# Six half output projections of a second transformer block, computed beside its attention heads instead of behind them

## The chip, the cores and the metric

One core of a Trainium2 chip runs the whole program. The metric is the device time of one execution in microseconds (us). Times shown for whole runs are medians over executions; times of single instructions come from one profiled execution.

## What is computed

The kernel computes two transformer blocks, of two layers each, over 512 tokens of 1024 features (256 further tokens in a context). What the change touches is the second block's `mixer_out`. Per layer:

```
px = split_cols(hx @ w_in[l])
q = rope_2d(px[0]...); k = rope_2d(px[1]...); v = px[2]
attn = windowed_attention(q, k, v, kc, vc, attn_sink[l])
...
y_conv = conformer_conv(c_a, c_b, conv_w, conv_b, ln_g, ln_b)
y_four = fourier_mix(f_u, w_four, b_four)
y = jnp.concatenate([attn * jax.nn.silu(g_att),        # 512 features: 8 heads of 64
                     y_conv * jax.nn.silu(g_conv),     # 256 features
                     y_four * jax.nn.silu(g_four)], axis=-1)  # 256 features
...
x = x + gate[:, None, :] * (y @ w_out)                 # 1024 -> 1024
```

The attention is over 128-token blocks with their neighbours and the 256 context tokens. In the tail of layer 0 the next layer's context keys and values are also made.

## The kernel before, in words

Activations lie transposed: a tile is 128 features by 512 tokens, so `x` is 8 tiles (`x_135` to `x_142` in the trace) and the concatenated `y` is 8 tiles, `ys[0..3]` from attention (two heads to a tile), `ys[4:6]` from the convolution, `ys[6:8]` from the Fourier part. Every value is kept as a high and a low part (hi, lo), and each product is three matmuls on TensorE (PE): hi by hi (L172), lo by hi (L173), hi by lo (L174). A weight chunk comes by a DMA on SyncE's queue into a `raw` tile (2 buffers). Each 1024 columns of it are then copied into `wh` on ScalarE (ACT, L146), and the rest is subtracted into `wl` on VectorE (DVE, L149); `wh` and `wl` have 3 buffers each.

`layer2` runs twice (l = 0 and 1). After the projections it runs the eight heads, `attn_x`. A head goes through scores (`z` banks), softmax on DVE and ACT, transposes of the probabilities (L1467), the split of these into `pt` hi (ACT) and `pt` lo (DVE), and value products (`b<-pt,Vh` and `b<-pt,Vl`). These steps are 48, and behind step i `more(i)` draws `FILL[i % 6]` steps from a generator, `rest()`, which holds work that doesn't depend on the heads: two gate projections, the Fourier projection, the end of the convolution, and the Fourier transform. It has 20 steps, and FILL gives 24 draws. What a draw emits stands at that place of the program; a scheduler then orders instructions on each engine by a model of the times, and each engine runs its own list in order.

Behind the heads stands `late()` (layer 0: the norm of the context) and then the output projection, `out_proj`. It takes `w_out` in four chunks c of 1 MB. Each gives two outputs j (one tile of `x` each), as 8 inputs by 3 matmuls of 512 columns, and the sum is added to `x` by `upd`, one DVE instruction (L156, `x<-b,ada_c,x`). The inputs come in the order 4, 5, 6, 7, 0, 1, 2, 3. The last chunk runs by halves of the tokens, beside the norm that follows (`ending`); in layer 0 also the next layer's context keys and values (`mid`, `ctx_kv`) are put ahead of it.

Of the kernel before, what the change touches and what calls it, by code (L numbers as in the profile page):

```python
# [15 lines left out]
ALU = mybir.AluOpType  # L16
# [18 lines left out]
FILL = (1, 0, 1, 0, 1, 0)  # L35
# [43 lines left out]
def body(ctx, tc, t, dbg):  # L79
# [55 lines left out]
    # work beside the main line comes behind this instruction of the vector engine  # L135
# [25 lines left out]
    def split(hi, lo, src, scale=None, eng=None):  # L161
        """hi + lo = src * scale; both fit one pass of the tensor engine."""
        if scale is None:
            copy(hi, src)
            tt(lo, src, f(hi), ALU.subtract, eng)
        else:
            copy(hi, src, scale)
            stt(lo, src, scale, f(hi), ALU.mult, ALU.subtract)
# [9 lines left out]
    def warm(n):  # L178
        """Products that nothing reads: they hold the tensor engine's clock up over a short wait."""
# [27 lines left out]
    def wjoin(srcs, n):  # L207
        """The same of several pieces of n columns one behind the other, 1024 columns to a tile."""
# [74 lines left out]
    # masks [q, k]: all; keys after the query; keys at or before it; keys after it. bef: keys before it  # L283
# [39 lines left out]
    def mod_dots(src, pairs, tag="m"):  # L323
        """pairs: (vector, destination column); src: [128, 1024] rows of a transposed weight."""
# [27 lines left out]
    def mods_first(ks):  # L352
        """The first shift and scale, tile by tile."""
# [44 lines left out]
    def rsqrt(v, n):  # L398
        """1 / sqrt(v) of a few columns: a first guess from the bits, and three Newton steps."""
# [10 lines left out]
    def rsqrt_ln(v, n):  # L410
        """1 / sqrt(v): a first guess by exp and ln, and a Newton step."""
# [8 lines left out]
    def rsqrt_act(src, n, over):  # L420
        """1 / sqrt(src / over + eps): a first guess by exp and ln, and a Newton step."""
# [9 lines left out]
    def colsum(tiles, n, fill=0):  # L431
        """sums over the partitions and tiles, tokens on the partitions: [128, n / 128] in PSUM."""
# [9 lines left out]
    def squares(tiles, n, eng=gp):  # L442
        """squares summed over the tiles but the last, and those of the last."""
# [12 lines left out]
    def spread(cols_, n):  # L456
        """[tokens, n / 128] -> [128, n], the same on every partition."""
# [20 lines left out]
    def norm_mod(xs, n, A, sh, dst, sq=None, cols_=None):  # L478
        """dst[k] = (hi, lo) of x * rsqrt(mean x^2 + eps) * A + sh."""
# [16 lines left out]
    class Ending:  # L496
        """The norm of X by halves of the tokens, beside the products that end the phase before."""
# [19 lines left out]
        def pace(self, d, i, at):  # L517
            """The first half's statistics go between the second half's products."""
# [4 lines left out]
    def modulated(A, sh):  # L523
        """An ending that leaves h, and its tiles."""
# [32 lines left out]
    def ffn(l, gu, dn, js, ji, per_f, per_d, h=None, sq=None, first=(), side=None, ending=None):  # L557
# [40 lines left out]
        if ending:  # L598
            # the last two outputs together, by halves of the tokens
# [18 lines left out]
    def positions():  # L618
# [8 lines left out]
        # angles, reduced to [-pi, pi]  # L627
# [18 lines left out]
        # distance of the one key that each merged column stands for: own block up to the query,  # L646
        # the block before past it
# [61 lines left out]
    def proj_gen(src, h, n, done):  # L709
        """The same step by step, handed to done at the end."""  # L710
# [11 lines left out]
    def proj_n(srcs, h, width, ntt):  # L722
        """token-major: [tokens, width] per 128 tokens."""
# [23 lines left out]
    def vtile(p):  # L747
        """hi and lo of a pair's values [keys, first | zeros | second], by 128 keys."""
# [5 lines left out]
    def v_evac(v, i, src, scale=None):  # L754
        """src [128, 128]: two heads of 64 go to columns 0 and 128 of 192."""
# [23 lines left out]
    def stick(r, q, k, v, po):  # L779
        """One head, half r of a pair: q, k (hi, lo) [128, 512]; scores as [key, query]."""  # L780
        rr = slice(r * 64, r * 64 + 64)
        za, zb, zc = (bank("z") for _ in range(3))
        # key block -> bank, its place there, and in the split parts
# [91 lines left out]
    def window_out(p, S, v, O):  # L875
        # transposed, by key block: queries of the same block, then of the next one
# [29 lines left out]
    def latent_proj(l, g, w3, cq, ckv, skv, ekv, kper, v, qk):  # L906
        """Queries and keys of two heads, normed and rotated; their values into v."""
# [63 lines left out]
    def latent_scores(q, k):  # L971
        """The probabilities of one head: by query block, over the keys up to it."""
# [17 lines left out]
    def latent_probs(E):  # L990
        """Transposed: by key block (hi, lo) over the queries from it on."""
# [22 lines left out]
    def rope(x, cg, sg, nh):  # L1014
        """x: [128, 2, nh, 32] in place; cg, sg: [128, 2, 32]."""
# [22 lines left out]
    def group_norm(O, l, base, over, mix):  # L1038
        """mix[i]: (hi, lo) made over the outputs themselves."""
# [8 lines left out]
    def out_proj(src, l, y, n, ks, after, upd, cs=range(4), ending=None, mid=None):  # L1048
        """ks: the inputs in the order in which they come; no weight is fetched before `after` is issued."""
# [24 lines left out]
    def mixer(l, h, ending):  # L1074
# [5 lines left out]
        def nb():  # L1080
            # values and window keys, token-major
# [22 lines left out]
        def sp(p):  # L1104
            # stick-breaking queries and keys, transposed
# [20 lines left out]
        def na():  # L1126
            # window queries and the shared rotated key part, token-major
# [503 lines left out]
    def layer2(l, rot, kc, vc, side, late, h, ending, mid=None):  # L1631
# [84 lines left out]
        def upd(d, ps, c):  # L1716
            stt(X[d][:, c], ps, MOD2[l, 2, "c2"][:, d:d + 1], X[d][:, c], ALU.mult, ALU.add)
# [189 lines left out]
```

## Time and profile before

| | us |
|---|---|
| median of 3 runs | 2899.38 |
| lowest and highest run | 2892.01, 2900.29 |
| span of the profiled execution | 2898.8 |
| PE busy in it (14059 instructions) | 2767.1 (95%) |
| weight loads of PE (PEld, overlapping PE) | 2332.3 (80%) |
| DVE busy | 1820.6 (63%) |
| ACT busy | 1151.5 (40%) |
| POOL busy | 511.9 (18%) |

The span is that of one execution under the profiler, and lies 0.6 us under the median. A busy share is over the whole span; what binds in one stretch is read from that stretch.

### The profile page before, as it was taken

How to read it: one execution, taken by the hardware profiler on the slowest of the kernel's cores; microseconds unless marked ns; L12 is line 12 of the kernel's file. 1: busy time of each engine (PE TensorE's matmuls, PEld its weight loads, DVE VectorE, ACT ScalarE, POOL GpSimd, SP SyncE). 2: the span in 40 equal slices, each digit the busy share in tenths (PEclk: the TensorE clock that was granted, in tenths of full speed). 3: DMA queues.
4: the chain of work that ended last, by engine and by line, in shares of the span. 5: the costliest groups of instructions: out<-in, count | busy, mean ns of one | idle time of the engine just before them, and what ended most of it. 6: DMA issues, size and time to landing. Idle time of an engine off the chain costs nothing.

```text
span 2898.8 us, 37037 instructions
## 1 busy us (share of the span) xinstructions
PE 2767.1 (95%) x14059; PEld 2332.3 (80%) x14059; DVE 1820.6 (63%) x3330; ACT 1151.5 (40%) x2231; POOL 511.9 (18%) x663
## 2 busy tenths in 40 slices
PE   7989999989999999999999899999999999999998
PEld 5767888778888888888888778888888977787776
DVE  7898965466666647743344766833487956559554
ACT  3333425655422334222345654222336234442352
POOL 3153411243000011000112421000012022211220
PEclk9999999979999999999999899999999988999899
DMA  7623362003467644532220023632233411122001
GB/s 266 222 82 107 128 236 75 29 8 117 162 239 247 234 164 137 186 123 102 80 97 29 15 95 124 223 104 102 84 128 105 150 36 36 59 88 73 35 30 58
DMA packets 69873, 334.40 MB, mean 115 GB/s; under 512 B 7872, under 2 KB 12224, under 8 KB 50112
## 3 DMA queue, kind: packets, MB, share of 16 engines
q1 hardware_dynamic: 69696, 332.05, 33.2%
q8 instruction: 110, 1.80, 0.2%
q14 instruction: 67, 0.55, 0.1%
HBM read 327.30 MB, written 4.72 MB: 115 GB/s over the span
## 4 chain that ended last, share of the span: by engine, by line
PE 79%; DVE 12%; ACT 3%; DMA 3%; issue 2%; POOL 0%; SPq 0%; DVEq 0%; POOLq 0%; ACTq 0%
PE b L173 17%; PE b L172 17%; PE b L174 17%; PE z L172 8%; PE z L174 7%; PE z L173 7%; DVE bacc L156 3%; DMA mraw<-wmod 3%; DVE wl L149 2%; PE z L438 1%; DVE mraw L156 1%; ACT s L129 1%; PE b L1467 1%; PE z L816 1%; DVE s L156 1%
## 5 line engine op out<-in xcount | busy, mean ns | idle before, releaser
L146 ACT ACTIVATE wh<-raw 128x1024 fp32r<-128x1024 f32 (+4 forms) x451 | 437.1, 972 | 756.3 <-PE b L173 365.0
L172 PE MATMUL b<-hh,wh 128*128 128x512 f32 (+1 forms) x1856 | 687.7, 378 | 17.6 <-DVE s L149 5.0
L174 PE MATMUL b<-hh,wl 128*128 128x512 f32 (+1 forms) x1856 | 693.3, 376 | 4.9 <-DVE wl L149 4.9
L149 DVE TENSOR_TENSOR wl<-raw,wh 128x1024 fp32r<-128x1024 f32 (+3 forms) x431 | 495.2, 1150 | 302.1 <-ACT wh L146 293.7
L173 PE MATMUL b<-hl,wh 128*128 128x512 f32 (+1 forms) x1742 | 668.4, 385 | 6.5 <-DVE hl L156 5.7
L172 PEld LDWEIGHTS b<-hh,wh 128*128 128x128 f32 x1856 | 348.7, 190 | 82.2 <-DVE s L149 5.5
L174 PEld LDWEIGHTS b<-hh,wl 128*128 128x128 f32 x1856 | 353.2, 190 | 68.6 <-DVE wl L149 7.4
L173 PEld LDWEIGHTS b<-hl,wh 128*128 128x128 f32 x1742 | 331.5, 190 | 71.9 <-DVE hl L156 8.8
L149 POOL TENSOR_TENSOR s<-s,s 128x512 f32<-128x512 f32 (+3 forms) x74 | 91.8, 1242 | 1178.6 <-ACT s L447 1070.5
L156 DVE SCALAR_TENSOR_TENSOR mraw<-mraw,c 128x1024 f32<-128x1024 f32 x192 | 236.7, 1244 | 86.6 <-DMA mraw<-wmod 80.4
L174 PE MATMUL z<-a,wl 128*128 128x512 f32 x638 | 251.3, 395 | 12.3 <-DVE wl L149 12.3
L172 PE MATMUL z<-a,wh 128*128 128x512 f32 x638 | 249.8, 393 | 3.2 <-ACT a L146 3.0
L173 PE MATMUL z<-a,wh 128*128 128x512 f32 x638 | 250.1, 393 | 0.0
L172 PE MATMUL b<-a,wh 128*128 128x256 f32 (+1 forms) x480 | 155.3, 326 | 8.1 <-ACT wh L146 6.7
L129 ACT ACTIVATE s<-b 128x512 f32<-128x512 f32 x87 | 51.8, 596 | 277.2 <-PE b L174 277.2
L174 PE MATMUL b<-a,wl 128*128 128x256 f32 (+1 forms) x480 | 155.2, 327 | 0.4 <-POOL wl L149 0.2
L174 PEld LDWEIGHTS z<-a,wl 128*128 128x128 f32 x638 | 120.9, 190 | 42.5 <-DVE wl L149 17.6
L149 DVE TENSOR_TENSOR s<-s,b 128x512 f32<-128x512 f32 x87 | 59.5, 684 | 136.7 <-PE b L174 117.5
L172 PEld LDWEIGHTS z<-a,wh 128*128 128x128 f32 x638 | 121.0, 190 | 28.7 <-ACT a L146 4.0
L173 PE MATMUL b<-a,wh 128*128 128x256 f32 (+1 forms) x440 | 140.5, 320 | 1.9 <-DVE a L149 1.9
L173 PEld LDWEIGHTS z<-a,wh 128*128 128x128 f32 x638 | 120.9, 189 | 25.4
L153 POOL TENSOR_SCALAR s<-s,tiny 128x256 f32<-128x256 f32 (+1 forms) x160 | 89.1, 572 | 285.0 <-DVE tiny L1376 133.2
(366 smaller groups left out, 5071.4 us busy)
## 6 DMA issues: line engine op xcount, KB each, us to landing
raw<-gu SPq DMA_DIRECT2D x88, 1024.0 KB, 4.9
mraw<-wmod SPq DMA_DIRECT2D x144, 512.0 KB, 4.7
raw<-dn SPq DMA_DIRECT2D x64, 704.0 KB, 4.2
raw<-wt SPq DMA_DIRECT2D x27, 1024.0 KB, 4.9
mraw<-wada SPq DMA_DIRECT2D x48, 512.0 KB, 4.0
raw<-wout SPq DMA_DIRECT2D x20, 1024.0 KB, 5.0
raw<-wq SPq DMA_DIRECT2D x6, 1024.0 KB, 5.0
raw<-wnb SPq DMA_DIRECT2D x4, 1024.0 KB, 4.9
```

The lines of the kernel that those rows point to most:

```text
L129: i = act_eng.activation(out, in_, func, **kw)
L146: return act_eng.activation(out, in_, AF.Copy, scale=scale)
L149: return (eng or dve).tensor_tensor(out=out, in0=a, in1=b, op=o)
L153: (eng or dve).tensor_scalar(out=out, in0=a, scalar1=s1, scalar2=s2, op0=o1, **kw)
L156: return dve.scalar_tensor_tensor(out=out, in0=a, scalar=s, in1=b, op0=o0, op1=o1, **kw)
L172: pe.matmul(out, wh, xh, start=start, stop=False, **kw)
L173: pe.matmul(out, wh, xl, start=False, stop=False, **kw)
L174: lastmm[0] = pe.matmul(out, wl, xh, start=False, stop=stop, **kw)
L438: lastmm[0] = pe.matmul(ps[:, i:i + 1], a[:, i * 128:(i + 1) * 128], one, start=m + i == 0, stop=True, skip_group_check=True)
L816: pe.matmul(b[:, c], ntri if jj == j else nones, a, start=False, stop=True, skip_group_check=True)
L1467: last = pe.transpose(pt[:, n * 128:n * 128 + 128], src, ident)
```

## The change

`FILL` becomes (1, 0, 1, 0, 1, 1), so that 32 draws are made. `rest()` gets 7 more steps. One is empty. The other 6 are the part of chunks c = 0, 1, 2 of the output projection that belongs to inputs 4 to 7 (convolution and Fourier tiles): for each c one load of 512 KB, one hi copy and one lo subtraction of 1024 columns, and for each of two outputs 12 matmuls and an `upd` of its own. Behind the heads `out_proj` takes only inputs 0 to 3 for these chunks (loads of 512 KB, one copy and one subtraction each); chunk 3 stays as it was. Comments and docstrings are removed as well, which moves line numbers and nothing else.

```
-FILL = (1, 0, 1, 0, 1, 0)
+FILL = (1, 0, 1, 0, 1, 1)
...
             yield from fourier_gen(l, fu, 512, gates[2:4], ys[6:8], "dft512",
                                    lambda i: (hslot("h", i % 4), hslot("l", i % 4)))
+            yield
+
+            for c in range(3):
+                w = wload(t["wout2"][l * 4 + c][:, 1024:2048], [(0, 1024)])[0]
+                for j in range(2):
+                    ps = bank()
+                    for i in range(4):
+                        mm3(ps, cut(w, slice(None), slice(i * 256 + j * 128, i * 256 + j * 128 + 128)), ys[4 + i],
+                            i == 0, i == 3)
+                    upd(2 * c + j, ps, slice(None))
+                    yield
+
+        def upd(d, ps, c):
+            stt(X[d][:, c], ps, MOD2[l, 2, "c2"][:, d:d + 1], X[d][:, c], ALU.mult, ALU.add)
 
         fill = rest()
...
         run(fill)
-
-        def upd(d, ps, c):
-            stt(X[d][:, c], ps, MOD2[l, 2, "c2"][:, d:d + 1], X[d][:, c], ALU.mult, ALU.add)
-
         late()
-        out_proj("wout2", l, ys, 512, (4, 5, 6, 7, 0, 1, 2, 3), after, upd, ending=ending, mid=mid)
+        out_proj("wout2", l, ys, 512, (0, 1, 2, 3), after, upd, (0, 1, 2))
+        out_proj("wout2", l, ys, 512, (4, 5, 6, 7, 0, 1, 2, 3), after, upd, (3,), ending=ending, mid=mid)
```

How this moves instructions is seen at three places, all in layer 1 (in layer 0 they read alike). The first is PE's list between the value products of head 5 (`b_23484` before, `b_23560` after) and the transposes of a later head. Before:

```order
L173 MATMUL b_23484<-pt_23700,Vh_3887_21772 128x384
L174 MATMUL b_23484<-pt_23700,Vl_3888_21773 128x384
L1467 MATMUL b_23852<-ident,s_23564 128x128
L1467 MATMUL b_23852<-ident,s_23605 128x128 x2
L1467 MATMUL b_23852<-ident,s_23632 128x128
L172 MATMUL b_23484<-pt_23722,Vh_3887_21772 128x384
```

After (`b_23896` and `b_23973` are the fourth and the fifth of the six new groups of 12 matmuls):

```order
L173 MATMUL b_23560<-pt_23847,Vh_3896_21790 128x256
L174 MATMUL b_23560<-pt_23847,Vl_3897_21791 128x256
L174 MATMUL b_23896<-a_4129_23273,wl_23856 128x512
L172 MATMUL b_23896<-a_4131_23275,wh_23855 128x512
L173 MATMUL b_23896<-a_4132_23276,wh_23855 128x512
L174 MATMUL b_23896<-a_4131_23275,wl_23856 128x512
L172 MATMUL b_23973<-a_4123_23255,wh_23969 128x512
L173 MATMUL b_23973<-hl_4124_23256,wh_23969 128x512
```

Twelve products of 512 columns follow one another for each new group, where transposes and value products alternated. All six groups stand ahead of the last value product of the last head.

The second place is DVE's list in the same stretch. Before (`pt` are lo halves of probabilities, `tiny` pieces of softmax sums, `s<-b` a pair of heads' output times its gate):

```order
L149 TENSOR_TENSOR pt_23722<-b_23718,pt_23722 128x384
L149 TENSOR_TENSOR pt_23731<-b_23728,pt_23731 128x256
L149 TENSOR_TENSOR pt_23857<-b_23852,pt_23857 128x512
L156 SCALAR_TENSOR_TENSOR s_23737<-b_23484,a_3977_22445 128x512
L149 TENSOR_TENSOR tiny_23752<-tiny_23752 128x1
```

After:

```order
L156 SCALAR_TENSOR_TENSOR x_136<-b_23820,ada_2_c_15444,x_136 128x512
L149 TENSOR_TENSOR pt_23838<-b_23834,pt_23838 128x384
L149 TENSOR_TENSOR pt_23847<-b_23844,pt_23847 128x256
L156 SCALAR_TENSOR_TENSOR x_137<-b_23859,ada_2_c_15444,x_137 128x512
L156 SCALAR_TENSOR_TENSOR s_23873<-b_23560,a_3986_22463 128x512
L149 TENSOR_TENSOR tiny_23888<-tiny_23888 128x1
L156 SCALAR_TENSOR_TENSOR x_138<-b_23896,ada_2_c_15444,x_138 128x512
```

Each group's `upd` stands among them; that of group 2 stands ahead of two lo halves of probabilities, and waits for its group's last product.

The third place is ACT's list where the heads end: the last hi copies of probabilities (`pt`), the copy of the last attention tile (`a<-s`), and the copies of weights. Before:

```order
L146 ACTIVATE pt_23987<-b_23983 128x384
L146 ACTIVATE pt_23996<-b_23993 128x256
L146 ACTIVATE a_4277_24004<-s_24002 128x512
L146 ACTIVATE wh_24010<-raw_24008 128x1024
L146 ACTIVATE wh_24014<-raw_24008 128x1024
```

After:

```order
L146 ACTIVATE pt_24107<-b_24103 128x384
L146 ACTIVATE pt_24116<-b_24113 128x256
L146 ACTIVATE wh_24130<-raw_24128 128x1024
L146 ACTIVATE a_4301_24124<-s_24122 128x512
L146 ACTIVATE wh_24164<-raw_24162 128x1024
```

The first product behind the heads reads `wh_24014` before, the second copy behind the attention tile's, and `wh_24130` after, which stands ahead of that tile's copy. On PE the first four products behind the heads read `wh`, and the fifth reads `wl`, before and after. In layer 0 one more place changes: before, the remaining products of chunk 2 and the warming products stood between the last use of the weight buffer that `ctx_kv` takes and `ctx_kv`'s first product; after, that product stands directly behind the last product of chunk 2, which frees the buffer.

## Rows read from the trace of the kernel before

**Rows 1.** The profile's page: busy time by engine, and the chain that ended last.

```profile
PE 2767.1 (95%) x14059; PEld 2332.3 (80%) x14059; DVE 1820.6 (63%) x3330; ACT 1151.5 (40%) x2231; POOL 511.9 (18%) x663
...
PE 79%; DVE 12%; ACT 3%; DMA 3%; issue 2%; POOL 0%; SPq 0%; DVEq 0%; POOLq 0%; ACTq 0%
```

**Rows 2.** Windows: heads of layers 0 and 1, dense products, two like stretches.

```profile
core 0: us, PE busy (x) PEld busy (x) DVE busy (x) ACT busy (x) POOL busy (x), PEclk, DMA share, GB/s
2351.00:2509.00 158.00, 153.17 (x725) 119.93 (x724) 85.08 (x208) 70.97 (x184) 31.57 (x49) 0.86 0.08 28
...
2682.30:2833.50 151.20, 146.89 (x731) 115.33 (x730) 84.95 (x209) 70.28 (x184) 31.50 (x48) 0.91 0.09 30
...
2841.00:2869.00 28.00, 28.00 (x125) 23.21 (x124) 8.65 (x9) 7.71 (x10) 5.47 (x4) 1.00 0.17 63
...
2451.00:2461.00 10.00, 10.00 (x32) 7.37 (x32) 4.72 (x15) 2.77 (x9) 3.41 (x6) 0.50 0.00 1
2782.00:2792.00 10.00, 10.00 (x57) 7.65 (x57) 6.53 (x20) 5.51 (x19) 3.41 (x6) 0.97 0.00 0
```

**Rows 3.** Waits of PE during the heads of layer 0: total us, times, longest.

```profile
PE b L173 <- DVE pt L149: 1.9, 1, 1.9
PE b L172 <- ACT pt L146: 1.6, 4, 0.7
PE z L172 <- ACT s L129: 0.7, 2, 0.6
```

**Rows 4.** Timeline of PE around the end of the heads, layers 0 and 1.

```profile
2508.65 0.29 PE L174 MATMUL b<-pt,Vl 128*128 128x256 f32 x1
2512.28 0.50 PE L172 MATMUL b<-a,wh 128*128 128x512 f32 x1 [3.34 <-ACT wh L146]
...
2833.22 0.28 PE L174 MATMUL b<-pt,Vl 128*128 128x256 f32 x1
2836.84 0.52 PE L172 MATMUL b<-a,wh 128*128 128x512 f32 x1 [3.34 <-ACT wh L146]
```

**Rows 5.** Timeline of ACT where the heads of layer 0 end.

```profile
2506.81 0.84 ACT L146 ACTIVATE pt<-b 128x384 fp32r<-128x384 f32 x2 [0.65 <-PE b L1467]
2509.70 0.63 ACT L146 ACTIVATE a<-s 128x512 fp32r<-128x512 f32 x1 [2.05 <-DVE s L156]
2510.24 2.94 ACT L146 ACTIVATE wh<-raw 128x1024 fp32r<-128x1024 f32 x3
```

**Rows 6.** Timeline of DVE at the same place.

```profile
2507.34 0.89 DVE L149 TENSOR_TENSOR pt<-b,pt 128x384 fp32r<-128x384 f32 x2 [0.59 <-ACT pt L146]
2508.98 0.69 DVE L156 SCALAR_TENSOR_TENSOR s<-b,a 128x512 f32<-128x512 f32 x1 [0.75 <-PE b L174]
2511.31 3.73 DVE L149 TENSOR_TENSOR wl<-raw,wh 128x1024 fp32r<-128x1024 f32 x3 [1.64 <-ACT wh L146]
```

**Rows 7.** Groups by form, 2834 to 2882 (three) and heads of layer 0 (last).

```profile
L149 DVE TENSOR_TENSOR wl<-raw,wh 128x1024 fp32r<-128x1024 f32 x8 | 9.9, 1251 | 9.2 <-ACT wh L146 9.0
L146 ACT ACTIVATE wh<-raw 128x1024 fp32r<-128x1024 f32 x8 | 8.2, 1053 | 5.1 <-PE b L173 5.1
L156 DVE SCALAR_TENSOR_TENSOR x<-b,ada_c,x 128x512 f32<-128x512 f32 x6 | 4.5, 751 | 14.5 <-PE b L174 14.5
...
L149 DVE TENSOR_TENSOR pt<-b,pt 128x512 fp32r<-128x512 f32 x16 | 11.0, 685 | 9.1 <-ACT pt L146 8.8
```

**Rows 8.** DMA issues in 2430 to 2530: KB each, median us to landing.

```profile
raw<-wout SPq DMA_DIRECT2D x4, 1024.0 KB, 4.9
ctx<-ctx_d SPq DMA_DIRECT2D x2, 512.0 KB, 4.0
```

**Rows 9.** Timeline of PE, the first product of `ctx_kv` in layer 0.

```profile
2554.70 0.39 PE L172 MATMUL b<-hh,wh 128*128 128x256 f32 x1 [0.58 <-ACT wh L146]
```

## The prediction

> **What bounds the kernel now.** I read the page first: PE is busy 95% of the span and holds 79% of the chain that ended last [rows 1]. So the first question is what PE has to do and the second where it stands still. The change neither adds nor removes matmuls; it moves 144 of them (2 layers x 3 chunks x 2 outputs x 4 inputs x 3 products), all of 512 columns, from behind the heads to beside them. Such a move can only gain what PE loses in the heads now, or what it loses where the heads end.
>
> I read three views on that. The windows: the heads of layer 0 take 158.00 us with PE busy 153.17, those of layer 1 take 151.20 with 146.89 [rows 2]. So 4.83 and 4.31 us are plainly idle. The chain of waits says on what: in layer 0 one wait of 1.9 us on a lo half of probabilities (`pt`, DVE), four on hi halves (ACT, 1.6 together), two on exponentials (0.7) [rows 3]. The timeline where the heads end: the last value product starts at 2508.65 and runs 0.29, and the next product waits 3.34 us for a weight copy on ACT; layer 1 shows the same 3.34 [rows 4].
>
> Busy is not the same as full there. Behind the heads, 125 dense products take 28.00 us, 0.224 us each, with weight loads (PEld) busy 23.21, a share of 0.829, at a granted clock of 1.00. In the heads PEld is busy 119.93 of 158.00 (0.76) and 115.33 of 151.20 (0.76), at mean clocks of 0.86 and 0.91; one stretch of 10 us runs at 0.50, and a like stretch of layer 1 gets through 57 products instead of 32 at 0.97 [rows 2].
>
> **The change, part by part.**
>
> *Behind the heads* 144 products of 0.224 us go: −32.3 us. This is sure, since that stretch is full (PE busy 28.00 of 28.00).
>
> *Beside the heads* the same products come back, +32.3 us, less what the heads absorb. The lower bound is nothing: the visible waits lie where no group stands, or new ones replace them. The upper bound comes from the weight loads: at the dense stretch's share of 0.829, layer 0's loads would fit into 119.93 / 0.829 = 144.7 us and layer 1's into 115.33 / 0.829 = 139.1, which leaves 13.3 and 12.1 us, 25.4 together. I take the plainly idle time, 4.83 + 4.31 = 9.1 us. Not each of those waits will have a group in front of it: in layer 1's order the six groups stand close to one another, in the last third of PE's list of the heads. But that is where the 1.9 us wait lies, and groups of twelve dense products should also give back some of the stretches at half clock, which are not in the 9.1. More I don't take, because the dense groups go mostly to a part that already runs near full clock, where a product costs its 0.224.
>
> The Trainium skill, page "Perfetto Trace Analysis", section "Identifying the Most-Contended Engine", says that the busy share of matmuls is not a good measure of how near PE is to its limit, and that MFU and the busy share of weight loads are to be used. By the busy share the heads are 97% full and could take 9.1 us; by the page's measure they are at 0.76 against 0.83 and could take 25.4. The second is a rival below.
>
> *The wait where the heads end.* Now the chain is: last value product, output times gate on DVE (2508.98, 0.69), attention tile's copy on ACT (2509.70, 0.63), then two weight copies, 1.04 each as 2.94 us hold three with overlap [rows 5, 6], and the first product needs the second copy. After the change the first product needs one copy that stands ahead of the attention tile's. It can start when the last hi half of probabilities is done, 2506.81 + 0.84 = 2507.65 [rows 5], and takes 1.05 [rows 7]: 2508.70, before the last value product ends (2508.94). So four products run at once, 0.90 us, and the fifth waits for `wl` on DVE: 0.04 + 0.69 for the output times gate [rows 6] and 1.25 for the subtraction [rows 7], 1.98 − 0.90 = 1.1 us. A wait of 3.34 becomes 1.1: −2.2 twice, −4.4. It rests on the 512 KB being there; a load of that size lands in 4.0 us [rows 8], and its buffer is free as soon as the second of the three new loads beside the heads has been split, some groups earlier. If it is not there, the term is nothing.
>
> *`ctx_kv` in layer 0.* Its first product waits 0.58 for a weight copy now [rows 9]. After the change the buffer of that copy comes free two products before `ctx_kv`: 1.05 − 0.22 = 0.8 us at least, +0.3.
>
> *What I cost at nothing.* Each layer's heads get 3 weight copies on ACT (1.05), 3 subtractions on DVE (1.25) and 6 `upd` of 0.75 [rows 7]: 3.2 us on ACT, busy 70.97 of 158.00, and 8.3 us on DVE, busy 85.08 [rows 2]. The 6 further `upd` per layer are real work, 4.5 us, hidden as long as PE doesn't wait for DVE. The cover is that PE has other products in its list between an `upd`'s group and the value products that read a lo half behind that `upd`. If the cover is gone, a value product waits for the group's last product to be added and its own lo half to be made: 0.04 + 0.75 + 0.69 = 1.5 us a group [rows 6, 7]. DMA: three loads of 1 MB become six of 512 KB per layer; SyncE's queue has nothing else to issue in the heads but the loads of the same generator, and DMA engines are busy 8 to 9% of the time there [rows 2], so 4.0 instead of 4.9 us each [rows 8] is hidden. That more draws are made moves the older steps of the generator a little forward; no product is added by it.
>
> *Sum:* −32.3 + 32.3 − 9.1 − 4.4 + 0.3 = −13.2 us, against the profiled span of 2898.8: 2885.6. The median lies 0.6 over that span: 2886.2 us, −0.46%.
>
> **The rivals.**
>
> *The heads have no room.* PE's idle time stays as it is, because each group lands where PE had work, and what it displaces waits as before. For it: 97% busy, and groups next to one another. Against it: the wait of 1.9 us is for a lo half that stood behind softmax sums, and twelve products now stand about there. Then only the end counts, −4.4 + 0.3: 2894.7, as a run 2895.3. That is 0.14% faster, less than the 0.3% that a measurement of this kernel can tell from no change.
>
> *DVE becomes what PE waits for.* An `upd` waits for its group's last product, in order, and lo halves queue behind it. For it: DVE's list shows `upd` ahead of two lo halves, and lo halves already make PE wait 1.9 us once [rows 3]. Against it: DVE is idle 73 of 158 us, and PE's list has products of the next group between. If each of the 12 groups costs its 1.5 us and nothing is absorbed: 2894.7 + 17.8 = 2912.5, as a run 2913.1, slower by 0.47%. It decides from about 9 of the 12 groups on (−4.1 + 9 x 1.5 = +9.2 us, over 0.3%, which is 8.7).
>
> *The heads are as empty as their weight loads say.* The dense groups bring the clock to full and fill the pipeline, and 25.4 us are absorbed: 2898.8 − 25.4 − 4.1 = 2869.3, as a run 2869.9, −1.0%. For it: half-clock stretches like that of [rows 2] would vanish if PE has dense work in them. Against it: transposes and value products are short, and their loads may not overlap as well as in a dense stretch whatever stands between; and where layer 0 ran at 0.50, the like stretch of layer 1 ran at 0.97, so it is not the lack of work alone.
>
> **How the numbers follow.** The forecast (partly absorbed, 5 to 16 us of 25) gets 0.55, with its own range 2879 to 2890. No room gets 0.22, the empty heads 0.12, DVE in the way 0.11. The range reaches from the lower half of the third rival's time to a little past no room: 2874 to 2899. Faster by over 0.3% (below 2890.7) takes the forecast but for its upper end, and the third rival: 0.52 + 0.12 = 0.64. Within 0.3%: the rest of the forecast, no room, and a few groups' worth of DVE's waits: 0.28. Slower: 0.08, the last part of DVE in the way.
>
> **What will show it.** Right, if after the change the heads are longer by about 11 to 12 us each (158 to some 170, 151 to some 162), PE idle there falls under 2 us or its mean clock rises, the 1.9 us wait on `pt` lo is gone, and where the heads end PE runs four products, then waits 1.1 us for `wl`. No room: heads longer by 16 us each. DVE in the way: waits of PE on `pt` lo halves of 1 to 1.5 us, once per group. Empty heads: longer by 4 us only, clock near 1.00 and PEld share above 0.8. I am wrong altogether if the clock falls in the heads where it was full before: at 0.50 the stretch above did 32 products for 57, and 20 us of such a stretch cost some 9 us, as much as all that I take as absorbed.

## The result

The changed kernel takes 2865.75 us (median of 4 runs, 2864.03 to 2866.28); beside it the kernel before took 2899.84. The ratio is 0.9887, with a 95% interval from 0.9861 to 0.9913: faster by 1.1%, 25 to 40 us. A second set of runs on another chip gave 2866.5 us and 0.9913 (0.9890 to 0.9935). The forecast was 2886.2 us, range 2874 to 2899: the direction was right, the gain more than twice what was forecast, and the time lies under the range.

The page of the changed kernel, its first part:

```profile
span 2864.6 us, 37064 instructions
...
PE 2744.2 (96%) x14059; PEld 2319.6 (81%) x14059; DVE 1825.4 (64%) x3342; ACT 1150.9 (40%) x2231; POOL 511.0 (18%) x663
```

The same 14059 matmuls were busy for 2767.1 us before [rows 1] and are busy for 2744.2 now. Work that is only moved doesn't shrink; it runs faster. The windows of the changed kernel say where. In order: heads of layer 0, heads of layer 1, what lies behind layer 1's heads, what lies behind layer 0's (columns as in [rows 2]).

```profile
2351.70:2508.60 156.90, 154.66 (x798) 124.83 (x798) 90.40 (x216) 74.89 (x188) 31.42 (x49) 0.95 0.10 31
2664.00:2820.40 156.40, 154.41 (x803) 124.94 (x803) 90.59 (x217) 74.79 (x190) 31.39 (x48) 0.96 0.09 31
2820.40:2864.60 44.20, 33.72 (x208) 30.11 (x206) 21.05 (x40) 10.70 (x19) 7.47 (x5) 0.88 0.25 84
2508.60:2664.00 155.40, 149.34 (x843) 128.72 (x842) 122.19 (x213) 58.83 (x111) 30.62 (x32) 0.97 0.28 94
```

And the two stretches behind the heads before the change, layer 1 and layer 0, in the same view:

```profile
2833.50:2898.80 65.30, 52.10 (x281) 44.99 (x280) 24.53 (x43) 15.12 (x23) 7.21 (x5) 0.89 0.19 65
2509.00:2682.30 173.30, 165.24 (x914) 142.04 (x915) 125.13 (x215) 63.71 (x115) 29.68 (x32) 0.97 0.25 86
```

The heads of layer 0 hold 73 matmul records more than before [rows 2] and take 156.90 us instead of 158.00; those of layer 1 hold 72 more and take 156.40 instead of 151.20. So 32.3 us of products came in and the heads grew by 4.1: 28.2 us were absorbed. Behind the heads 17.9 and 21.1 us went. With 0.7 us of a later start the sum is the −34.2 us between the two spans.

What was absorbed is seen in two columns. Idle time of PE (length less busy) fell from 4.83 and 4.31 to 2.24 and 1.99, by 4.9 us. And the granted clock rose from 0.86 and 0.91 to 0.95 and 0.96. At a granted clock of 0.50 ("half clock", 1.2 of 2.4 GHz) products of 512 columns start 0.43 us apart in the kernel before, at 1.00 they start 0.23 us apart. So time lost to half clock can be worked out as (1 − clock) x length: it was 22.1 and 13.6 us and is 7.8 and 6.3, 21.6 us less. 4.9 + 21.6 = 26.5 of 28.2; the rest is within the rounding of the clock to hundredths. This compares one profile with one profile; what the runs as a whole say stands behind the experiments.

The waits of PE in the heads of layer 0 after the change (total us, times, longest), where [rows 3] showed one of 1.9 us:

```profile
PE b L172 <- ACT pt L146: 0.7, 1, 0.7
PE b L173 <- DVE pt L149: 0.5, 2, 0.3
PE z L172 <- ACT s L129: 0.5, 1, 0.5
PE b L1467 <- DVE hl L149: 0.3, 1, 0.3
```

The timeline of PE where the heads end, layers 0 and 1, and at the first product of `ctx_kv`; these answer to [rows 4, 9].

```profile
2508.29 0.29 PE L174 MATMUL b<-pt,Vl 128*128 128x256 f32 x1
2508.42 0.39 PE L172 MATMUL b<-a,wh 128*128 128x512 f32 x1
...
2510.57 0.50 PE L174 MATMUL b<-a,wl 128*128 128x512 f32 x1 [1.08 <-DVE wl L149]
...
2822.30 0.50 PE L174 MATMUL b<-a,wl 128*128 128x512 f32 x1 [1.09 <-DVE wl L149]
...
2533.92 0.39 PE L172 MATMUL b<-hh,wh 128*128 128x256 f32 x1 [0.92 <-ACT wh L146]
```

The first products run as soon as the last value product is issued, and the fifth waits 1.08 and 1.09 us for its `wl`, where 1.1 was forecast. `ctx_kv` waits 0.92, where 0.8 was.

### The profile page after: what moved, and what is told of

Read it like the earlier page. It is cut to its first block, busy times and chain, and to the rows that moved or that the text cites. A ratio compares the mean times of both kernels' runs of the same rounds, so it can differ in the third digit from the quotient of the medians.

```text
span 2864.6 us, 37064 instructions
## 1 busy us (share of the span) xinstructions
PE 2744.2 (96%) x14059; PEld 2319.6 (81%) x14059; DVE 1825.4 (64%) x3342; ACT 1150.9 (40%) x2231; POOL 511.0 (18%) x663
## 4 chain that ended last, share of the span: by engine, by line
PE 77%; DVE 13%; DMA 4%; ACT 3%; issue 2%; POOL 1%; SPq 0%; DVEq 0%; POOLq 0%; ACTq 0%
PE b L173 16%; PE b L172 16%; PE b L174 16%; PE z L172 8%; PE z L174 7%; PE z L173 7%; DVE bacc L156 3%; DMA mraw<-wmod 3%; DVE wl L149 2%; DVE mraw L156 2%; PE z L438 2%; DMA mraw<-wada 1%; PE b L1467 1%; PE z L816 1%; ACT s L129 1%
## 5 line engine op out<-in xcount | busy, mean ns | idle before, releaser
L173 PEld LDWEIGHTS z<-a,wh 128*128 128x128 f32 x638 | 120.9, 189 | 25.4
```

The source lines that it names most:

```text
L173: pe.matmul(out, wh, xl, start=False, stop=False, **kw)
```

## Where half clock came from

Two views of the kernel before show what PE did before its granted clock fell. First, stretches in the windows: one ahead of a fall and one behind it in the heads of layer 1, and one behind the wait of 3.34 us where layer 0's heads end.

```profile
2747.80:2751.80 4.00, 4.00 (x18) 2.37 (x16) 2.99 (x9) 1.91 (x4) 0.73 (x2) 1.00 0.00 0
2751.90:2758.60 6.70, 6.70 (x18) 4.61 (x18) 1.37 (x4) 2.71 (x10) 0.69 (x1) 0.50 0.00 0
...
2512.90:2516.30 3.40, 3.27 (x9) 2.06 (x8) 2.14 (x2) 2.73 (x9) 2.36 (x2) 0.50 0.36 87
```

The third is the plain case: PE stood still for 3.34 us and, 0.6 us after it went on, ran at half clock. The first two are not: PE was busy 4.00 of 4.00 us at full clock, and then ran at half clock for 6.70 us, again with no gap. The groups of the first stretch, by form, say with what it was busy:

```profile
L172 PE MATMUL z<-a,a 64*128 64x384 f32 x2 | 0.9, 442 | 0.0
L173 PE MATMUL b<-hl,wh 128*128 128x512 f32 x2 | 0.8, 394 | 0.0
L173 PE MATMUL z<-kc,a 64*128 64x256 f32 x2 | 0.7, 332 | 0.0
L172 PE MATMUL z<-kc,a 64*128 64x256 f32 x2 | 0.7, 329 | 0.0
L173 PE MATMUL b<-pt,Vh 128*128 128x384 f32 x1 | 0.6, 570 | 0.0
L174 PE MATMUL z<-kc,a 64*128 64x256 f32 x2 | 0.6, 278 | 0.0
```

Ten of the 18 are score products of 64 rows and 256 or 384 columns (`z<-a,a`, `z<-kc,a`); 4 have 512 columns. This is what PE did before the fall, not what set the fall off: since 2732 it had been busy for at least 1.99 of every 2 us with products of the same kinds, at a clock of 1.00. After the change the clock doesn't fall where the heads end, with 1.08 and 1.09 us of waiting (windows of the changed kernel):

```profile
2509.00:2512.50 3.50, 2.42 (x11) 1.67 (x10) 2.99 (x3) 2.81 (x6) 2.42 (x3) 1.00 0.94 317
2820.40:2824.00 3.60, 2.51 (x11) 1.78 (x10) 3.06 (x3) 1.58 (x2) 1.53 (x1) 1.00 0.25 40
```

## The experiments

Theory A: products of 512 columns among the short ones of the heads hold the granted clock up, and what they save there is the part of the gain that the forecast lacks. Rival B: it is FILL, that is the new spacing of the older steps (gates, Fourier) beside the heads. Each run is compared with runs of the kernel before on the same chip (medians 2895 to 2897 us). "Clock" of a run is the mean over the whole span; "lost" below is (1 − mean clock) x median time.

**FILL alone.**

```
-FILL = (1, 0, 1, 0, 1, 0)
+FILL = (1, 0, 1, 0, 1, 1)
```

> The kernel before with the new FILL alone; no product is moved. Theory A (the moved dense products keep the granted clock of TensorE up in the heads, and that is where 20 of the 33 us come from): the heads stay as they were, 158 and 151 us within 4 us, and the whole run stays at 2893 to 2901 us. Rival B (it is the new spacing of the older steps beside the heads that removes the stretches at half clock): the heads fall by 10 to 14 us each, and the run to 2872 to 2880 us.

Measured: 2884.0 us (2873.7 to 2890.1), ratio 0.9953 (0.9930 to 0.9977). The windows of its heads:

```profile
2351.50:2505.80 154.30, 150.65 (x725) 120.69 (x724) 83.22 (x207) 70.81 (x184) 31.42 (x49) 0.86 0.08 28
2680.40:2819.90 139.50, 135.59 (x723) 108.76 (x722) 83.77 (x207) 70.63 (x184) 31.30 (x48) 0.96 0.09 31
```

Neither expectation held: the run lies between them. Layer 0 keeps its clock of 0.86, layer 1 goes to 0.96. The spacing alone is worth 0.5%, 11 us (7 to 20 by the interval), which is some 40% of the gain in the first set of runs and half of that in the second, and A alone is refuted.

**The change with the old FILL** (24 draws, so the last steps are emitted behind the heads).

```
-FILL = (1, 0, 1, 0, 1, 1)
+FILL = (1, 0, 1, 0, 1, 0)
```

> The change with the old FILL: the products are moved, but the last three of the seven new steps are emitted behind the last step of the heads, and the groups stand late. Theory A: the groups crowd into the last two heads, so stretches at half clock that lie earlier in the heads stay; between 8 and 20 us of the 32 are absorbed, and the run takes 2872 to 2885 us. Rival B (spacing of the older steps): with the old spacing the heads absorb their idle time of some 9 us only, and the run takes 2884 to 2892 us.

Measured: 2881.1 us, 0.9940 (0.9921 to 0.9959), inside A's range. Moving the products without the spacing is worth 0.6%, and 0.6 and 0.5 add up to the whole. It is not a clean half, though: in this run's profile the late groups also stand where PE waited when the heads end, and PE doesn't stand still there in either layer, where the changed kernel waits 1.08 and 1.09 us.

**Unread products at the same places, nothing removed** (in `rest()` of the kernel before, with the new FILL).

```
+            yield
+            for c in range(3):
+                for j in range(2):
+                    ps = bank()
+                    for i in range(4):
+                        yh, yl = ys[4 + i]
+                        for m, x in enumerate((yh, yl, yh)):
+                            pe.matmul(ps, identr, x, start=i + m == 0, stop=i + m == 5)
+                    yield
```

> The kernel before with the new FILL, and at the places of the six new groups of a layer 12 products of 512 columns that nothing reads, of a constant tile against the convolution and Fourier tiles: no load, no split, no update, and nothing is taken away behind the heads. 144 products, 32.3 us at 0.224, are added to the program. Theory A: the heads take about as long as after the change (157 us each), so that the run takes 2899 to 2907 us in spite of them. If the heads have no room for products (the gain would come from elsewhere), they take 16 us more each, and the run 2925 to 2933 us.

Measured: 2905.1 us, 1.0028 (1.0009 to 1.0046), inside A's range. The windows of its heads:

```profile
2347.30:2510.20 162.90, 161.24 (x798) 129.37 (x796) 83.52 (x208) 71.74 (x184) 31.40 (x49) 0.91 0.08 27
2685.40:2837.90 152.50, 150.75 (x796) 121.28 (x795) 83.62 (x208) 71.57 (x184) 31.28 (x48) 0.98 0.08 28
```

32.3 us of useless products made the heads 6.2 us longer than before, and the whole run by 0.28%, about 8 us. So the heads absorb products as such, whatever is taken away behind them. Against FILL alone they cost 21 us of 32.3, so 11 are absorbed.

The same two profiles show where. The stretch at the end of the heads, layers 0 and 1, in which the groups stand: FILL alone, then with the unread products, then the changed kernel.

```profile
2474.00:2505.80 31.80, 29.45 (x142) 23.72 (x140) 17.29 (x43) 16.69 (x46) 7.82 (x13) 0.79 0.01 2
2792.00:2819.90 27.90, 25.36 (x132) 20.21 (x130) 16.43 (x41) 15.42 (x41) 7.69 (x12) 0.88 0.00 1
...
2470.20:2510.20 40.00, 39.64 (x212) 31.99 (x210) 17.25 (x44) 17.31 (x45) 7.93 (x13) 1.00 0.01 2
2797.90:2837.90 40.00, 39.62 (x212) 31.94 (x210) 17.22 (x44) 17.26 (x44) 7.76 (x12) 1.00 0.00 1
...
2469.50:2508.60 39.10, 38.87 (x213) 32.10 (x212) 22.45 (x50) 19.31 (x48) 7.85 (x13) 1.00 0.05 16
2781.20:2820.40 39.20, 38.97 (x214) 32.15 (x214) 22.49 (x50) 19.34 (x48) 7.78 (x12) 1.00 0.04 14
```

With the products the clock is 1.00 there, read or unread; without them it is 0.79 and 0.88, which costs 6.7 and 3.3 us, and PE is idle for 4.9 us instead of 0.7. Ahead of the groups none of the 144 products stands. The kernel before has no groups; it is cut here at the last 31 us of its heads, and those are the two last lines. The part ahead, before and after:

```profile
2351.00:2478.00 127.00, 124.81 (x577) 96.72 (x576) 66.28 (x169) 55.12 (x147) 26.77 (x41) 0.84 0.08 26
2682.30:2802.00 119.70, 117.98 (x579) 91.76 (x578) 65.74 (x171) 53.62 (x146) 26.82 (x41) 0.90 0.08 29
...
2351.70:2469.50 117.80, 115.79 (x587) 92.74 (x587) 67.95 (x167) 55.58 (x141) 23.57 (x36) 0.93 0.11 37
2664.00:2781.20 117.20, 115.43 (x591) 92.79 (x591) 68.10 (x168) 55.45 (x143) 23.61 (x36) 0.94 0.11 37
...
2478.00:2509.00 31.00, 28.36 (x150) 23.21 (x149) 18.81 (x40) 15.85 (x38) 4.80 (x8) 0.94 0.11 37
2802.00:2833.50 31.50, 28.91 (x153) 23.57 (x152) 19.21 (x39) 16.66 (x38) 4.68 (x7) 0.95 0.10 34
```

So most of the 21.6 us of the profiled pair lies where only older steps were shifted (32.3 us lost before, 15.3 after; with FILL alone 18). How much is the shift and how much the run can't be told from two profiles: with the changed kernel's order in that part the same loss was 12 us in its second profile and 24 in the profile without updates (both below).

**One chunk, two chunks, four chunks moved.** In the first two the other chunks stay behind the heads with all eight inputs; in the third, chunk 3 is moved like the others and runs behind the heads with inputs 0 to 3, and the place of the next norm's statistics among its products is set anew. The cut shows the first.

```
-            for c in range(3):
+            for c in range(1):
...
-        out_proj("wout2", l, ys, 512, (0, 1, 2, 3), after, upd, (0, 1, 2))
-        out_proj("wout2", l, ys, 512, (4, 5, 6, 7, 0, 1, 2, 3), after, upd, (3,), ending=ending, mid=mid)
+        out_proj("wout2", l, ys, 512, (0, 1, 2, 3), after, upd, (0,))
+        out_proj("wout2", l, ys, 512, (4, 5, 6, 7, 0, 1, 2, 3), after, upd, (1, 2, 3), ending=ending, mid=mid)
```

> The change for chunk 0 alone: two groups per layer beside the heads, chunks 1 and 2 behind them as before. Behind the heads 48 products go, 10.8 us, and 4.4 us of the waits where the heads end. Theory A: two groups already break some of the stretches at half clock, so the heads stay as long as they were or get shorter, and the run takes 2875 to 2886 us. If the gain goes in proportion to the products: a third of the 28 us in the heads, the run 2884 to 2888 us.

> The change for chunks 0 and 1: four groups per layer beside the heads. With the new FILL alone 0.47% was gained, with one chunk moved 0.82%, with three 1.13%. Theory A (the first groups win most, since they take the stretches at half clock away, and later ones cost their full price): two chunks come close to three, 0.95 to 1.15%. If every chunk brings the same: 0.9%.

> The changed kernel with the same part of chunk 3 moved too: eight groups per layer beside the heads, 48 products of 512 columns' worth fewer behind them (10.8 us). Theory A: the heads now run at 0.95 to 0.96 of the clock with 2 us idle, so nearly nothing is left to absorb; the heads grow by 4.5 to 5.4 us each and the run stays within 4 us, 2862 to 2869. If the heads still have room as before the change, another 6 to 9 us are gained: 2857 to 2860.

Measured: one chunk 2875.4 us, 0.9918 (0.9890 to 0.9946), at the edge of A's range; two 2871.6, 0.9924 (0.9898 to 0.9951), a median under both expectations; four 2869.7, 0.9927 (0.9900 to 0.9955), a little beyond A's range. Windows of the heads with one chunk:

```profile
2356.90:2504.30 147.40, 144.71 (x751) 116.10 (x751) 85.63 (x210) 72.90 (x186) 31.36 (x49) 0.94 0.09 30
2671.10:2818.30 147.20, 144.63 (x750) 116.25 (x750) 86.50 (x210) 73.28 (x186) 31.26 (x48) 0.94 0.09 29
```

With 24 products more per layer the heads are 10.6 and 4.0 us shorter than before. From here to three chunks (156.90 and 156.40) 48 more products per layer cost 9.5 and 9.2 us, 0.19 to 0.20 each, nearly their price; against the changed kernel's second profile (152.50 and 157.80, below) they cost 5.1 and 10.6, so the price is not settled. The first chunk, with the spacing, takes most of the gain; between one, two, three and four the intervals overlap. That two come as close to three as A says is neither shown nor refuted.

**A little unread work in the kernel before, old FILL** (in `more(i)`, 4 products behind every sixth step, 64 in the program).

```
+            if i % 6 == 5:
+                a = getattr(lastmm[0], "ins", lastmm[0])
+                ps = bank()
+                for _ in range(4):
+                    m = pe.matmul(ps, identr, swm, start=True, stop=True)
+                    order(getattr(m, "ins", m), a)
```

> The kernel before with its old FILL, and 4 products of 512 columns that nothing reads behind every sixth step of the heads: 64 in the program, 14.3 us at 0.224. No older step is moved in the program. Theory A: they shorten the stretches at half clock in the heads (44 and 27 us before) by about as much as they cost, and the run stays within 5 us of the kernel before. Rival B (only the spacing of the older steps matters): the run gets 12 to 15 us longer, 0.4 to 0.5%.

Measured: 2896.1 us, 1.0008 (0.9982 to 1.0034). 14.3 us of products cost nothing that can be measured (the interval is 5 us less to 10 us more). The heads in its profile, which is one of its faster runs:

```profile
2358.10:2505.20 147.10, 142.29 (x755) 111.83 (x755) 83.57 (x208) 71.14 (x184) 31.89 (x49) 0.99 0.09 30
2679.80:2824.70 144.90, 141.48 (x753) 111.81 (x753) 84.73 (x208) 71.20 (x184) 31.70 (x48) 0.99 0.09 30
```

Seven of a layer's eight groups of 4 stand in the heads (30 and 22 records more, since some are missing in a trace), the last behind the last value product, where PE then waits 2.42 us instead of 3.34. The heads are 10.9 and 6.3 us shorter than before, at a clock of 0.99. No older step of the program was moved. This shows A's mechanism by itself: dense products among the short ones pay for most of their price through the clock (some 10 us in the table below), and for a little of it in the wait where the heads end. (The other runs of this kernel had a mean clock of 0.969 against 0.972 in the profiled one, so 0.99 is its good case.)

**The same in the changed kernel**, all over the heads, and only behind the third and the sixth step.

> The changed kernel with 4 products that nothing reads behind every sixth step of the heads, the places at which they cost the kernel before nothing: 64 in the program, 14.3 us. Theory A says that here they cost most of their price, since the moved products already hold the clock: at most the 7 to 17 us of half clock left per layer can be won, 3 to 8 us of time each. The run takes 2865 to 2875 us. Were they free here too, whatever the clock does, it would stay at 2864 to 2868.

> The changed kernel with 4 products of 512 columns that nothing reads behind the third and behind the sixth step of each layer's heads: 16 in the program, 3.6 us at 0.224. They stand at the two places at the start of the heads where half clock remains after the change (7 to 17 us a layer in its two profiles). Theory A (such products hold the granted clock): these stretches shrink by more than half, and the run is 3 to 8 us shorter than the changed kernel, 2858 to 2863 us. Rival (what is left there follows from a wait of TensorE, and products only shift it): 2866 to 2871 us.

Measured: all over the heads 2878.8 us, 0.9948 (0.9928 to 0.9968), 13 us over the changed kernel: here they cost nearly their price of 14.3, a little beyond what A allowed. The mean clock of these runs is the highest of all (0.973), and 8 us came back through it, as A allowed. But beside the clock the runs are 20 us longer, more than the products' price; 2 us of that is more idle time in the heads, the rest is open. At the start only: 2870.8 us, 0.9915 (0.9892 to 0.9938), no gain, as the rival says. In its profile the stretch at half clock at the start of layer 1's heads cost 1.7 us, where it cost 6.8 in the changed kernel, but the heads as a whole ran at 0.90:

```profile
2655.80:2822.50 166.70, 165.00 (x811) 132.94 (x811) 93.46 (x217) 74.88 (x189) 32.30 (x48) 0.90 0.09 29
```

Half clock came up in other places; in this profile a few products at one place held the clock there and nowhere else.

**Other spacings.** One draw behind each of the first six steps and then the old pattern; and the groups cut into steps of three products, one drawn behind every step.

```
-FILL = (1, 0, 1, 0, 1, 1)
+FILL = (1, 1, 1, 1, 1, 1) + 7 * (1, 0, 1, 0, 1, 0)
...
-            for _ in range(FILL[i % 6]):
+            for _ in range(FILL[i]):
```

```
-FILL = (1, 0, 1, 0, 1, 1)
+FILL = (1, 1, 1, 1, 1, 1)
...
                             i == 0, i == 3)
+                        if i < 3:
+                            yield
                     upd(2 * c + j, ps, slice(None))
                     yield
```

> The changed kernel with the 27 steps drawn earlier: one behind each of the first six steps of the heads, and then three in six as before the change, so that the last comes with the heads' end. Theory A (dense products between transposes and value products keep the clock up): what is left of half clock after the change lies at the start of each layer's heads (13.7 us in either layer), and products drawn there take it away: 8 to 13 us less, 2853 to 2858. Rival: that stretch follows a wait of TensorE at the first softmax and comes whatever is drawn, or the stretches come back later where fewer products stand: 2866 to 2880.

> The changed kernel with the moved groups cut finer: a step after every three products instead of after twelve, 45 steps in all, and one drawn behind each of the 48 steps of the heads. Theory A (512-column products among the short ones keep the granted clock up): with some in every step, stretches at half clock in the heads fall under 10 us per layer (17 and 14 after the change), and the run takes 2852 to 2864 us. Rival (the spacing of the change is near the best, and drawing the older steps this early leaves the last heads to short products): 2866 to 2880 us.

Measured: 2876.6 us, 0.9940 (0.9922 to 0.9959), and 2884.7 us, 0.9960 (0.9942 to 0.9979); the rival was right in the first and not hard enough in the second. The waits of PE in the heads of layer 0 with the finest spacing:

```profile
PE b L172 <- ACT pt L146: 3.5, 6, 1.0
PE b L173 <- DVE pt L149: 2.3, 3, 1.2
```

There the clock is 0.96, no higher than in the changed kernel, and PE waits 5.8 us for halves of probabilities. Idle time in the heads of both layers is 11.8 us instead of 4.2, which is 8 of the 18 us by which this run is longer than the change; the rest is open.

**Only the order of inputs**, in the kernel before.

```
-        out_proj("wout2", l, ys, 512, (4, 5, 6, 7, 0, 1, 2, 3), after, upd, ending=ending, mid=mid)
+        out_proj("wout2", l, ys, 512, (0, 1, 2, 3, 4, 5, 6, 7), after, upd, ending=ending, mid=mid)
```

> The kernel before, with the inputs of the output projection in the order 0 to 7 for all chunks, and nothing else: the first product behind the heads then reads the first weight copy, not the second, but that copy still stands behind the attention tile's on ScalarE. The prediction's term for the end of the heads: the wait of 3.34 falls by one copy, to 2.3 us, twice. If that is all, 2 us (0.07%) are gained, and that can't be told from no change in the whole run. If a shorter wait also keeps the clock from falling there (it ran at half clock for 3.4 us behind each of these waits before), another 1.7 us each.

Measured: 2892.9 us, 0.9994 (0.9972 to 1.0017). The wait of 3.34 is 2.39 in both layers, with 0.30 more four products later, near what was expected, and half clock still follows it.

**No updates beside the heads** (the six groups of a layer are computed and dropped).

```
-                    upd(2 * c + j, ps, slice(None))
                     yield
```

> The changed kernel without the 12 updates of x beside the heads, so the output lacks what the moved products give. The prediction costs them at nothing: the run then stays at that of the changed kernel within 3 us (2863 to 2869), with no wait of TensorE less. If updates ahead of lo halves hold up TensorE (the rival with 1.5 us a group), up to 18 us less: 2848 to 2860.

Measured: 2868.2 us, 0.9923 (0.9893 to 0.9952): no gain, as expected. The updates are hidden.

**The change again.**

> The changed kernel itself, on the same chip as the three others, as the measure for them; and a second profile of it. Theory A: mean granted clock in the heads again 0.94 to 0.97 in both layers, idle time of TensorE there 2 to 2.5 us, and the run 1.0 to 1.2% faster than before. If the first profile's clock was luck: 0.86 to 0.92 in one layer at least, and a run 0.5 to 0.9% faster.

Measured: 2866.5 us, 0.9913 (0.9890 to 0.9935). Windows of the heads:

```profile
2351.50:2504.00 152.50, 150.28 (x798) 120.95 (x798) 90.80 (x216) 74.79 (x188) 31.34 (x49) 0.98 0.10 32
2659.00:2816.80 157.80, 155.81 (x802) 125.89 (x802) 90.64 (x217) 74.73 (x190) 31.25 (x48) 0.95 0.09 31
```

The clock of the first profile was no luck on the whole, though a layer can come out lower: the profile without the updates shows 0.91 in layer 0. No other version that was tried is faster than the change.

Over all runs the mean granted clock splits the times in two:

| kernel | runs | median us | mean clock | lost to half clock | rest |
|---|---|---|---|---|---|
| before (beside the experiments) | 69 | 2896.4 | 0.9653 | 101 | 2796 |
| the change (both sets) | 8 | 2866.1 | 0.9706 | 84 | 2782 |
| FILL alone | 6 | 2884.0 | 0.967 | 94 | 2790 |
| unread at the same places | 10 | 2905.1 | 0.970 | 86 | 2819 |
| one chunk | 5 | 2875.4 | 0.969 | 90 | 2786 |
| little unread work, old FILL | 10 | 2896.1 | 0.969 | 90 | 2806 |
| the same in the changed kernel | 7 | 2878.8 | 0.973 | 76 | 2802 |

Of the change's 30 us over these runs, 16 to 17 are half clock and 14 are the rest. The profiled pair showed more of half clock (21.6) because the profiled execution of the kernel before had a mean clock of 0.962, under the 0.9653 of its runs.

By way of FILL alone the 30 us come in two parts, each good to some 3 us, for the clock of a run is known to a thousandth and runs differ. FILL takes 12: 6 of half clock and 6 of the rest, of which 1.6 is idle time in the heads. The moved products take 18 more: 10 of half clock, as much as FILL alone loses at the end of its heads, and 8 of the rest, of which 3.3 is idle time in the heads and 4.1 the waits behind them.

## Why the prediction was wrong, by its steps

*Behind the heads, −32.3.* Right: with the shorter waits the stretch between the heads of the two layers fell by 17.9 us, where 16.15 + 2.2 − 0.3 = 18.05 was forecast. Behind layer 1's heads 21.1 went instead of 18.35.

*The wait where the heads end, −4.4, and `ctx_kv`, +0.3.* Right in place and size: 3.34 became 1.08 and 1.09 (−4.5), 0.58 became 0.92. Left out: behind the long wait PE ran at half clock (the window 2512.90 to 2516.30 above, 1.7 us lost, and about as much in layer 1), and that went too. In layer 0 a later stretch at half clock grew by as much (3.4 to 5.1 us lost), so the forecast came out there in part by luck; in layer 1 it is most of the 2.8 us by which the end gained more.

*Work costed at nothing.* For the updates this is right: without them the kernel is not faster. For the draws it is the first step that failed: "That more draws are made moves the older steps of the generator a little forward; no product is added by it." No product is added, and yet FILL alone took 11 us off, nearly as much as the whole forecast and more than half of the 20 us by which it fell short. No row stood behind that term.

*Beside the heads, 9.1 us absorbed.* This is the second step that failed. 28.2 us were absorbed in the profiled pair: 15.4 with FILL alone (the heads 309.2 to 293.8 us) and 12.8 by the products (293.8 to 313.3 for 32.3 us of products; 11 by the unread ones over whole runs). For the products themselves 9.1 was not far off, but not for its reason: the plain idle time that the term was made of gave back 4.9 us, about half, and the clock gave the rest. "More I don't take, because the dense groups go mostly to a part that already runs near full clock": in the kernel before that was so, its last 31 us of either layer's heads ran at 0.94 and 0.95. But the older steps had 36 products of 512 columns there in layer 0 and 37 records in layer 1; with FILL alone 2 and none are left, and the clock is 0.79 and 0.88. The forecast read the clock of a part whose dense work the same change takes away. And it read it as if half clock had fixed places in the program; where it comes differs from run to run.

Without the clock the runs give −14, and the sum said −13.2. That is luck in good part: the sum took 9.1 us for idle time where 4.9 came, and some 5 us of FILL's gain, in neither idle time nor clock, fill the gap.

*The rivals.* Nearest was "the heads are as empty as their weight loads say", 2869.9 us at a chance of 0.12, with 25.4 us absorbed where 28.2 were. What was put against it, that layer 1 ran at 0.97 where layer 0 ran at 0.50, was taken the wrong way: that the same program shows both may mean that the clock there is close to falling, and that a little more dense work holds it; the unread products are in favour of this. The sign it named came true in the clock (0.95 and 0.96); the share of weight loads did not go above 0.8 (124.83 of 156.90 is 0.80), so the bound by weight loads came near by luck, for a reason that it doesn't contain, and with FILL's part in it. The measure that the Trainium skill, page "Perfetto Trace Analysis", section "Identifying the Most-Contended Engine", asks for instead of the busy share of matmuls gave the nearer figure here. What it says of the busy share the trace bears out: PE at 97% busy had 28 us to give. "DVE in the way" did not happen: no `pt` wait of over 0.7 us is left in the heads.

*The cause of the clock's rise* is in part the products (shown by the unread ones, twice) and in part the spacing of the older steps (FILL alone, 0.5%). How the spacing does it is not shown. Its profile fits the same mechanism: the older steps' dense products go forward out of the end of the heads, where the clock falls (0.94 and 0.95 to 0.79 and 0.88), to the part ahead, where it rises (0.84 and 0.90 to 0.87 and 0.98). And some 5 us of its gain are in neither the idle time nor the clock, which stays open.

## What to carry to other kernels

Where PE is near 100% busy but its granted clock is under 1, count (1 − clock) x length of the stretch as possible room, beside the idle time: dense products put among short ones there can cost nothing, as 14.3 us of them did in the kernel before. They need not: in the changed kernel the same ones cost nearly their price. Don't price at nothing a change that only shifts work which is there already: here it was worth 11 us. Finer cutting did not help: three products behind every step left PE idle in the heads for 8 us more, mostly in waits for halves of probabilities. And read the clock from several executions, for one profile's places of half clock are not those of the next.

## What was not expected of the hardware

The run-to-run spread of the kernel before is mostly the granted clock. In 21 runs on one chip the fastest took 2876.0 us at a mean clock of 0.972 and the slowest 2912.7 at 0.960; lost to half clock that is 80.5 and 116.5 us, 36 us apart, and the times are 36.7 apart. The changed kernel's 8 runs lie within 2862.3 to 2869.7, but a higher clock does not bring less spread by itself: with two chunks the mean clock was 0.971 and 6 runs lay within 20 us. And the clock fell in a stretch where the profile shows PE busy without a gap, mostly with score products of 64 rows; the like had run at full clock just before, so what set it off is open.
